# One set of four PSUM banks for the projections, the maxima and the down projection, in place of separate sets of one and three

## The chip, the cores and the metric

The kernel runs on one core of a Trainium2 chip. The metric is the device time in microseconds (us) of one execution. Names of the engines in this text: PE is TensorE's matmul queue (PEld is its weight load), DVE is VectorE, ACT is ScalarE, POOL is GpSimd, SP is SyncE, which issues the DMAs. The matmuls write to PSUM, of which there are eight banks here; a bank holds 128 x 512 fp32 values, and the engines that read it afterwards are DVE and ACT.

## The reference

One layer (DEPTH is 1) on 2048 tokens of width 1024:

```python
h = _modulate(x, ln1_g[l], sh1, sc1)
u = h @ w_in[l]
fq, fk, fv, fg, dq, dk, dv = jnp.split(u, splits, axis=-1)
...
fox_out = _fox_attention(fq, fk, fv, log_f)
...
diff_out = _diff_attention(dq[:, :, 0], dq[:, :, 1], dk[:, :, 0], dk[:, :, 1], dv, lam, slopes)
...
x = x + g1[:, None, :] * (mixed @ w_out[l])

h2 = _modulate(x, ln2_g[l], sh2, sc2)
y = (jax.nn.silu(h2 @ w_gate[l]) * (h2 @ w_up[l])) @ w_down[l]
x = x + g2[:, None, :] * y
```

Both attentions are causal and softmaxed; q and k are normalised per head. There are 8 heads of 64 in the first and 4 heads of two maps each in the second. The hidden width of the last product is 2816.

## The kernel before

**Precision.** Nearly every operand is split into two fp16 parts, a high and a low one, and each product is made as three matmuls (high x high, high x low, low x high) that add up in one bank.

**Start (about 0 to 150 us).** The modulation is computed, x is normalised block by block (16 blocks of 128 tokens), transposed on PE (L245, into banks of the tags "mx" and "st" in turn) and split into `hts`. The first blocks are projected (L451).

**Attention (about 150 to 1470 us).** There are eight groups: four differential ones, then four pairs of heads of the other kind. A group is 80 units; a unit is one block of 128 keys against 512 queries (`qc`, `kb`) of one of two maps `m`. For each unit `scores` writes to a bank "st" (L593, L594, and L596 for the mask), ACT takes the exponential out of it (L599) and copies it to fp16 (L604), POOL makes the low part (L607), and three units later (`PVLAG`) `weigh` multiplies with the values into a bank "pv" (L621 to L623). Ahead of the scores of a row of queries stand the maxima: `max_part` (L560) writes scores to a bank "mx", DVE reduces them (L562, or L564 on the diagonal), L569 makes the row `t_mrow`, L572 transposes it with four small matmuls and ACT puts it with the queries (L573).

**Between the units** PE projects for the next group: 16 blocks, each 24 matmuls into one bank "ip" (L451). ACT empties it in two copies (L452, L456) and DVE takes the low part of the values last (L144). During the last group it is the output projection that is done between the units (`out_proj`, L950, 24 matmuls into a bank, read by DVE in L952).

**Feed-forward (about 1600 us to the end).** In 22 rounds `product` makes seven products of 12 matmuls each for the gate and seven for the up weights (L1143, banks "st", "pv" and, for i = 6, "mx", which L1172 reads); `down` multiplies the round before with w_down, 6 matmuls into a bank "mx" (L1202), which DVE adds to the residual (L1206). Maxima over partitions are made with one matmul (`colmax`, L108, here into "ip") that DVE reduces (L109). Over the first ten rounds the rest of the normalised rows is made as well (`late_sum`). DVE also reduces each load of w_down (L1113).

**What sets the order.** The program is written as streams that are merged by weight (`run`). A scheduler then puts each engine's instructions into a fixed order; it gives a PSUM bank to a tile when one of its tag's set is free. On the chip every engine goes through its queue in that order and waits where an operand or a bank is not ready. So the number of banks of a tag acts twice: on the order that is written down, and on what is waited for.

Of the kernel before, what the change touches and what calls it, by code (L numbers as in the profile page):

```python
# [55 lines left out]
def trunk(ctx, tc, t):  # L56
# [5 lines left out]
    dram = ctx.enter_context(tc.tile_pool(name="dram", bufs=1, space=bass.MemoryType.DRAM))  # L62
    V, A, G, T = nc.vector, nc.scalar, nc.gpsimd, nc.tensor

    PSB = {"ip": 1, "st": 2, "pv": 2, "mx": 3}

    def bank(tag, dt=F32):
        n = 512 if dt == F32 else 1024
        return ps.tile([P, n], dt, tag=tag, bufs=PSB[tag], name=f"ps_{tag}")

    def small(n, tag, bufs=3, dt=F32):
# [28 lines left out]
    def colmax(am, tag=None):  # L100

        g = small(1, "cm", bufs=4)
        if tag is None:
            G.partition_all_reduce(g, am, channels=P, reduce_op=ReduceOp.max)
            return g

        b = bank(tag)
        T.matmul(b[:, 0:P], lhsT=am.broadcast_to([P, P]), rhs=idb, start=True, stop=True)  # L108
        V.tensor_reduce(out=g, in_=b[:, 0:P], op=ALU.max, axis=AX.X)  # L109
        return g  # L110
# [85 lines left out]
    def ada_columns(acc, q, ab):  # L196

        b = bank("ip")
        for i in range(KT):
            T.matmul(b[:, i : i + 1], lhsT=acc[:, i * P : (i + 1) * P], rhs=ones, start=(i == 0), stop=True, skip_group_check=True)  # L200
        bb = bada[:, q * KT : (q + 1) * KT]
        if q % 3 == 0:
            V.tensor_tensor(out=ab[:, KT:], in0=b[:, 0:KT], in1=bb, op=ALU.add)
        else:
            V.tensor_tensor(out=ab[:, 0:KT], in0=b[:, 0:KT], in1=bb, op=ALU.add)
            g = lng[:, (q // 3) * KT : (q // 3 + 1) * KT]
            V.scalar_tensor_tensor(out=ab[:, 0:KT], in0=ab[:, 0:KT], scalar=1.0, in1=g, op0=ALU.add, op1=ALU.mult)
# [29 lines left out]
    def to_hT(y, ab, s, ht, col, t32, tag="mx"):  # L237

        h = ht.bitcast(F16).rearrange("p (k s n) -> p k s n", k=KT, s=2)[:, :, :, col : col + P]
        t3 = t32.rearrange("p (k n) -> p k n", k=KT)  # L240
        for half in range(2):
            b = bank(tag)
            for i in range(4):
                k = half * 4 + i
                T.transpose(out=b[:, i * P : (i + 1) * P], in_=y[:, k * P : (k + 1) * P], identity=idf)  # L245
            for i in range(4):
                k = half * 4 + i
                if i < 3:
                    A.activation(t3[:, k, :], b[:, i * P : (i + 1) * P], AF.Identity, bias=ab[:, KT + k : KT + k + 1], scale=ab[:, k : k + 1])
                else:  # L250
                    V.tensor_scalar(out=t3[:, k, :], in0=b[:, i * P : (i + 1) * P], scalar1=ab[:, k : k + 1], scalar2=ab[:, KT + k : KT + k + 1], op0=ALU.mult, op1=ALU.add)
        cast_scaled("G", h[:, :, 0, :], t3, s)
        sub_scaled(h[:, :, 1, :], t3, s, h[:, :, 0, :])
# [1001 lines left out]
    for q in range(NQP + 1):  # L1255
        st = [[] for _ in range(14)]
# [109 lines left out]
```

## Time and profile before

| | |
|---|---|
| median of 3 runs | 2898.03 us (2892.18 to 2898.2) |
| profiled execution | 2903.69 us |
| its span | 2901.9 us |
| PE busy | 2717.1 us, 94% |
| DVE busy | 2143.8 us, 74% |
| ACT busy | 1436.7 us, 50% |
| POOL busy | 1655.5 us, 57% |

The span is what the profiler shows from the first to the last instruction; 1.8 us of the execution lie around it. A share is the time in which the engine had at least one instruction running. Matmuls overlap, so two that start 0.2 us apart can each last 0.4 us.

### The profile page before, as it was taken

What the parts mean: (1) busy time and instruction counts of PE and PEld (TensorE: products, weight loads), DVE (VectorE), ACT (ScalarE), POOL (GpSimd) and SP (SyncE); (2) the same over time, 40 slices, a digit from 0 to 9 for tenths busy, and PEclk for the clock granted to TensorE, in tenths of its full rate; (3) what the DMA queues carried; (4) which work ended last, traced back from release to release, by engine and by line L of the source; (5) the groups of instructions that cost most, each with busy time, mean ns of one, the idle gap of its engine ahead of it and who ended that gap; (6) DMA issues with size and microseconds to landing.
All of it is one profiled execution on the core that took longest, in us unless ns stands there. A gap on an engine that the chain in (4) does not pass through costs nothing. (4 is left out here: it accounts for less than half of the span.)

```text
span 2901.9 us, 49724 instructions
## 1 busy us (share of the span) xinstructions
PE 2717.1 (94%) x18924; PEld 1478.5 (51%) x18924; DVE 2143.8 (74%) x4195; ACT 1436.7 (50%) x2704; POOL 1655.5 (57%) x1392
## 2 busy tenths in 40 slices
PE   4899989899998999999899899999999999999999
PEld 3466656566665655665444344444444444444444
DVE  7786675867758686646766887878877787878785
ACT  4666667666676777786552432333323232333231
POOL 2566666665667787776552655555554545455541
PEclk9999999999999999999999999999999999999999
DMA  6332231322223244225678333333334511111111
GB/s 233 77 90 56 63 76 39 84 49 67 74 50 91 53 112 96 49 55 158 165 185 257 122 114 100 97 106 102 106 97 153 174 58 59 59 44 64 53 37 58
DMA packets 276816, 274.52 MB, mean 95 GB/s; under 512 B 205144, under 2 KB 221912, under 8 KB 270816
## 3 DMA queue, kind: packets, MB, share of 16 engines
q1 hardware_dynamic: 276576, 271.34, 33.2%
q8 instruction: 148, 2.42, 0.4%
q14 instruction: 92, 0.75, 0.1%
HBM read 181.94 MB, written 41.11 MB: 77 GB/s over the span
## 5 line engine op out<-in xcount | busy, mean ns | idle before, releaser
L607 POOL TENSOR_TENSOR pxs<-pxs 128x512 f16<-128x512 f32 (+3 forms) x640 | 685.1, 1085 | 333.1 <-ACT pxs L604 200.7
L451 PE MATMUL ps_ip<-wbuf,ht 128*128 128x384 f16 (+1 forms) x2952 | 563.2, 333 | 24.4 <-DVE vts L144 14.4
L1143 PEld LDWEIGHTS <-mt 128*128 128x128 f16 x3696 | 358.4, 98 | 437.2 <-issue 14.4
L1202 PE MATMUL ps_mx<-wide,ht 128*128 128x512 f16 x2112 | 505.5, 380 | 21.5 <-DVE mt L1206 16.1
L1087 POOL TENSOR_TENSOR pxm<-vts 128x512 f32<-128x512 f32 x220 | 342.5, 1588 | 211.0 <-DMA vts<-in_w_gu_dram 200.7
L599 ACT ACTIVATE pxs<-ps_st,cells 128x512 f32<-128x512 f32 (+3 forms) x640 | 388.7, 620 | 141.1 <-PE ps_st L594 69.4
L451 PEld LDWEIGHTS <-ht 128*128 128x128 f16 x3072 | 296.7, 100 | 241.5 <-issue 47.3
L1143 PE MATMUL ps_st<-ht,mt 128*128 128x512 f16 x1584 | 373.5, 379 | 0.1
L1143 PE MATMUL ps_pv<-ht,mt 128*128 128x512 f16 x1584 | 368.6, 379 | 0.0
L604 ACT ACTIVATE pxs<-pxs 128x512 f16<-128x512 f32 (+3 forms) x640 | 350.6, 565 | 18.9 <-PE ps_pv L623 10.2
L621 PE MATMUL ps_pv<-vts,pxs 128*128 128x129 f16 (+1 forms) x2176 | 342.2, 207 | 4.7 <-DVE os L640 3.7
L1202 PEld LDWEIGHTS <-ht 128*128 128x128 f16 x2112 | 205.2, 98 | 274.4 <-issue 25.2
L622 PE MATMUL ps_pv<-vts,pxs 128*128 128x128 f16 (+1 forms) x2176 | 344.2, 208 | 0.0
L623 PE MATMUL ps_pv<-vts,pxs 128*128 128x129 f16 (+1 forms) x2176 | 324.9, 206 | 7.7 <-POOL pxs L607 7.0
L562 DVE TENSOR_REDUCE t_mxc<-ps_mx 128x1 f32<-128x512 f32 x384 | 256.7, 682 | 91.1 <-PE ps_mx L560 89.5
L1206 DVE SCALAR_TENSOR_TENSOR mt<-ps_mx,t_ai,mt 128x512 f32<-128x512 f32 x352 | 256.3, 742 | 34.2 <-PE ps_mx L1202 34.0
L621 PEld LDWEIGHTS <-pxs 128*128 128x128 f16 x2176 | 207.9, 97 | 56.8 <-ACT pxs L599 3.5
L593 PE MATMUL ps_st<-mt 67*128 67x512 f16 (+7 forms) x640 | 223.5, 350 | 11.3 <-ACT pxs L599 10.9
L623 PEld LDWEIGHTS <-pxs 128*128 128x128 f16 x2176 | 206.6, 99 | 45.7 <-POOL pxs L607 18.5
L622 PEld LDWEIGHTS <-pxs 128*128 128x128 f16 x2176 | 207.7, 97 | 35.7 <-issue 4.5
L594 PE MATMUL ps_st<-mt 128*128 128x512 f16 (+3 forms) x640 | 223.3, 349 | 0.0
L560 PE MATMUL ps_mx<-mt 71*128 71x512 f16 (+7 forms) x640 | 197.1, 349 | 17.2 <-DVE t_mxc L562 12.5
(262 smaller groups left out, 4136.6 us busy)
## 6 DMA issues: line engine op xcount, KB each, us to landing
vts<-in_w_gu_dram SPq DMA_DIRECT2D x44, 1024.0 KB
stg<-in_w_down_dram SPq DMA_DIRECT2D x44, 512.0 KB
stg<-in_w_ada_dram SPq DMA_DIRECT2D x32, 512.0 KB
stg<-in_w_in_dram SPq DMA_DIRECT2D x24, 512.0 KB
stg<-yd SPq DMA_DIRECT2D x48, 256.0 KB
mt<-in_w_ada_dram SPq DMA_DIRECT2D x16, 512.0 KB
mt<-mt SPq DMA_DIRECT2D x128, 64.0 KB
mixed<-os SPq DMA_DIRECT2D x32, 256.0 KB
```

The lines of the kernel that those rows point to most:

```text
L451: T.matmul(pt[:, 0:N], lhsT=h4[:, k, hs, c : c + P], rhs=w4[k // 4][:, k % 4, ws, 0:N], start=(i == 0), stop=(i == len(terms) - 1))
L562: V.tensor_reduce(out=mx[:, 4 * j + n : 4 * j + n + 1], in_=b[:, 0:w], op=ALU.max, axis=AX.X)
L599: A.activation(p32[:, c0:QC], b[:, c0:QC], AF.Exp, bias=pshift, scale=1.0)
L604: A.activation(ph[:, c0:QC], p32[:, c0:QC], AF.Copy, bias=0.0, scale=1.0)
L607: (V if hilo[1] == "V" else G).tensor_tensor(out=pl[:, c0:QC], in0=p32[:, c0:QC], in1=ph[:, c0:QC], op=ALU.subtract)
L621: T.matmul(pv[:, jj, :], lhsT=lhs_h, rhs=v4[:, kb, h, 0 : W + 1], start=first, stop=False, skip_group_check=True)
L622: T.matmul(pv[:, jj, 0:W], lhsT=lhs_h, rhs=v4[:, kb, h, W + 2 : 2 * W + 2], start=False, stop=False, skip_group_check=True)
L623: T.matmul(pv[:, jj, :], lhsT=lhs_l, rhs=v4[:, kb, h, 0 : W + 1], start=False, stop=end, skip_group_check=True)
L1087: G.tensor_tensor(out=sums[:, k * 512 : (k + 1) * 512], in0=raw[:, a * 512 : (a + 1) * 512], in1=raw[:, b * 512 : (b + 1) * 512], op=op)
L1143: T.matmul(b.rearrange("p (b n) -> p b n", b=4), lhsT=aw[w][:, APOS[i] * 4 + k, ws, :], rhs=cb[:, :, 2 * k + hb, :], start=(fresh and k == ...
L1202: T.matmul(b, lhsT=aT[:, th, as_, f, j * P : (j + 1) * P], rhs=dnb[:, (2 * q + f) % 4, ws, n * 512 : (n + 1) * 512], start=(f == 0 and z = ...
L1206: V.scalar_tensor_tensor(out=xs, in0=b, scalar=sets[q]["ai", th], in1=xs, op0=ALU.mult, op1=ALU.add)
```

## The change

The bank table loses the tags "ip" (one bank) and "mx" (three) and gains "any" (four); `bank` maps every tag that the table does not have to "any". The tags "st" and "pv" keep their two banks each, so all eight banks are in use before and after. No instruction is added or removed; all lines below L65 move down by one.

```diff
-    PSB = {"ip": 1, "st": 2, "pv": 2, "mx": 3}
+    PSB = {"any": 4, "st": 2, "pv": 2}
 
     def bank(tag, dt=F32):
         n = 512 if dt == F32 else 1024
+        tag = tag if tag in PSB else "any"
         return ps.tile([P, n], dt, tag=tag, bufs=PSB[tag], name=f"ps_{tag}")
```

The scheduler writes another order for every engine. Three places follow.

**PE at the start**, from the matmul that gives the bound of the modulation to the first projection (`ht` is the normalised block at L245 and the transposed one at L451). Before:

```order
L108 LDWEIGHTS t_amh
L108 MATMUL ps_mx<-idb,t_amh 128x128
L245 MATMUL ps_mx<-idf,ht 128x128 x8
L451 LDWEIGHTS ht
L451 MATMUL ps_ip<-wbuf,ht 128x392
```

After:

```order
L109 LDWEIGHTS t_amh
L109 MATMUL ps_any<-idb,t_amh 128x128
L246 MATMUL ps_any<-idf,ht 128x128 x8
L246 MATMUL ps_st<-idf,ht 128x128 x8
L246 MATMUL ps_any<-idf,ht 128x128 x8
L452 LDWEIGHTS ht
L452 MATMUL ps_any<-wbuf,ht 128x392
```

The transposes of the second and third block stood behind 16 and 19 matmuls of the first projection, and now stand ahead of it.

**PE in the attention** of the fourth group (qc = 1, the second map), at the scores of its third to fifth block of keys; the numbers are those of the tiles, the same in both orders. Before, from the score tile 9536:

```order
L451 MATMUL ps_ip_9741<-wbuf_100,ht_239 128x384
L593 LDWEIGHTS mt_7152
L593 MATMUL ps_st_9536<-mt_7152 128x512
L594 LDWEIGHTS mt_7152
L594 MATMUL ps_st_9536<-mt_7152 128x512
L560 LDWEIGHTS mt_7149
L560 MATMUL ps_mx_9518<-mt_7149 128x512
L593 LDWEIGHTS mt_7152
L593 MATMUL ps_st_9573<-mt_7152 128x512
```

After, from the same tile to the start of 9618, the next one:

```order
L594 MATMUL ps_st_9536<-mt_7152 128x512
L595 LDWEIGHTS mt_7152
L595 MATMUL ps_st_9536<-mt_7152 128x512
L594 LDWEIGHTS mt_7152
L594 MATMUL ps_st_9573<-mt_7152 128x512
L595 LDWEIGHTS mt_7152
L595 MATMUL ps_st_9573<-mt_7152 128x512
L594 LDWEIGHTS mt_7152
L594 MATMUL ps_st_9618<-mt_7152 128x512
```

Before, the two matmuls of 9573, three of the maxima and 12 of the weighting stand between the scores 9536 and 9618, two tiles apart on a set of two banks; now only the two matmuls of 9573 do.

**DVE in the feed-forward**, around the reduction of the first load of w_down for the twelfth round (`t_dam<-stg`); the lines after the change are higher by one. Before:

```order
L1157 TENSOR_TENSOR uhm<-ps_st,uhm 128x512
L1206 SCALAR_TENSOR_TENSOR mt<-ps_mx,t_ai,mt 128x512 x2
L1166 TENSOR_TENSOR mt<-ps_pv,pxm 128x512
L1113 TENSOR_REDUCE t_dam<-stg 128x1
L1206 SCALAR_TENSOR_TENSOR mt<-ps_mx,t_ai,mt 128x512
L123 TENSOR_REDUCE t_amh<-uhm 128x1
L1206 SCALAR_TENSOR_TENSOR mt<-ps_mx,t_ai,mt 128x512
L109 TENSOR_REDUCE t_cm<-ps_ip 128x1
```

After:

```order
L1158 TENSOR_TENSOR uhm<-ps_st,uhm 128x512
L1207 SCALAR_TENSOR_TENSOR mt<-ps_any,t_ai,mt 128x512 x2
L1167 TENSOR_TENSOR mt<-ps_pv,pxm 128x512
L1114 TENSOR_REDUCE t_dam<-stg 128x1
L1207 SCALAR_TENSOR_TENSOR mt<-ps_any,t_ai,mt 128x512
L124 TENSOR_REDUCE t_amh<-uhm 128x1
L1207 SCALAR_TENSOR_TENSOR mt<-ps_any,t_ai,mt 128x512
L110 TENSOR_REDUCE t_cm<-ps_any 128x1
```

Nothing moved here; only the set of banks is another.

## Rows read from the trace of the kernel before

**Rows 1.** The page: the span and the busy times of the engines.

```profile
span 2901.9 us, 49724 instructions
...
PE 2717.1 (94%) x18924; PEld 1478.5 (51%) x18924; DVE 2143.8 (74%) x4195; ACT 1436.7 (50%) x2704; POOL 1655.5 (57%) x1392
```

**Rows 2.** Busy time by stretch: length, the engines, granted clock, DMA share, GB/s.

```profile
60.00:150.00 90.00, 72.86 (x466) 45.21 (x465) 67.97 (x178) 58.66 (x163) 51.59 (x52) 0.92 0.26 66
...
300.00:1300.00 1000.00, 941.98 (x9147) 611.09 (x9144) 692.08 (x1710) 695.98 (x1500) 679.13 (x696) 0.98 0.29 69
1300.00:1670.00 370.00, 334.69 (x2326) 166.53 (x2325) 260.08 (x408) 185.85 (x342) 199.24 (x154) 0.97 0.64 176
1670.00:2310.00 640.00, 616.62 (x2860) 277.39 (x2859) 515.48 (x807) 201.32 (x236) 335.50 (x209) 0.99 0.38 117
2310.00:2902.00 592.00, 585.87 (x2747) 266.41 (x2744) 457.08 (x730) 173.02 (x193) 277.57 (x167) 1.00 0.16 55
```

**Rows 3.** What PE waited for: us in total, times, longest.

```profile
PE ps_ip L200 <- DVE ht L194: 22.9, 2, 14.1
PE ps_mx L1202 <- DVE mt L1206: 16.1, 18, 2.2
PE ps_mx L572 <- DVE t_mrow L569: 15.6, 11, 2.5
PE ps_ip L451 <- DVE vts L144: 14.4, 14, 2.9
PE ps_ip L950 <- DMA wide<-wide: 13.0, 5, 6.8
PE ps_mx L560 <- DVE t_mxc L562: 12.5, 20, 1.6
...
PE ps_st L593 <- ACT pxs L599: 10.9, 17, 2.1
...
PE ps_mx L1143 <- DVE mt L1206: 5.0, 3, 3.9
PE ps_ip L950 <- DVE uhm L952: 4.7, 5, 1.9
...
PE ps_mx L560 <- DVE t_mxc L564: 3.3, 2, 3.0
PE ps_ip L950 <- DVE ht L952: 3.3, 4, 1.8
```

**Rows 4.** DVE in order of time around 2180 us: start, us, instruction, [idle before].

```profile
2172.82 0.67 DVE L1166 TENSOR_TENSOR mt<-ps_pv,pxm 128x512 f32<-128x512 f32 x1
2180.60 1.22 DVE L1113 TENSOR_REDUCE t_dam<-stg 128x1 f32<-128x1024 f32 x1 [7.10 <-DMA stg<-in_w_down_dram]
2181.74 0.74 DVE L1206 SCALAR_TENSOR_TENSOR mt<-ps_mx,t_ai,mt 128x512 f32<-128x512 f32 x1
...
2184.18 0.28 DVE L109 TENSOR_REDUCE t_cm<-ps_ip 128x1 f32<-128x128 f32 x1
```

**Rows 5.** PE in order of time in the feed-forward, at three places.

```profile
1741.81 2.72 PE L1202 MATMUL ps_mx<-wide,ht 128*128 128x512 f16 x6 [2.21 <-DVE mt L1206]
...
1780.80 1.45 PE L1202 MATMUL ps_mx<-wide,ht 128*128 128x512 f16 x6 [1.15 <-DVE mt L1206]
...
2171.70 2.75 PE L1202 MATMUL ps_mx<-wide,ht 128*128 128x512 f16 x12
2174.28 0.22 PE L108 MATMUL ps_ip<-idb,t_amh 128*128 128x128 bf16 x1
```

**Rows 6.** The start in order of time, PE and POOL.

```profile
43.04 5.41 PE L451 MATMUL ps_ip<-wbuf,ht 128*128 128x392 f16 x16 [5.79 <-POOL ht L141]
...
43.56 3.27 POOL L235 TENSOR_SCALAR ht<-ht,t_nr 128x1024 f32<-128x1024 f32 x2 [0.57 <-DVE t_eps L379]
...
48.24 1.27 PE L245 MATMUL ps_st<-idf,ht 128*128 128x128 f32 x8
```

**Rows 7.** The attention's score tiles from 300 to 1300 us, in groups.

```profile
L599 ACT ACTIVATE pxs<-ps_st,cells 128x512 f32<-128x512 f32 (+1 forms) x483 | 294.1, 620 | 102.5 <-PE ps_st L594 44.5 <-PE ps_pv L623 24.2 <-PE ps_st L596 20.9
```

## The prediction, made before the changed kernel was run

> **What bounds the kernel now.** I read the page first, then busy time by stretch, PE's list of waits, the order of time at the longest waits, and the written order of both kernels. PE runs for 94% of the span and no other engine above 74% [rows 1], so PE is the bound, and what a change of banks can give back is PE's idle time: 2901.9 - 2717.1 = 184.8 us. By stretch [rows 2]: in the attention 58 of 1000 us (300 to 1300), around the output projection 35 of 370, in the first half of the feed-forward 23 of 640, in its second half 6 of 592. That half runs almost without gaps at the full granted clock (1.00); in the other stretches the clock averages 0.92 to 0.99, so some matmuls also ran at 1.2 GHz instead of 2.4.
>
> The waits name what can be freed [rows 3]. Waits for a bank, that is for the reader of an older tile: 16.1 + 5.0 us for L1206 in the feed-forward, 14.4 us for L144 (a projection's only bank), 12.5 + 3.3 us for the maxima's L562 and L564, and 4.7 + 3.3 us for L952 after an output projection. That is 59 us. Waits that no bank of this set removes: 22.9 us at the start, 15.6 us for the row `t_mrow`, 13.0 us for transposes by DMA, and 10.9 us of score matmuls for the exponential that still reads their "st" bank.
>
> **The change part by part.** Counts of instructions and durations stay; banks and order change. The whole effect is in which gaps close and which open. I sum against the profiled execution, 2903.69 us, which is 5.66 us above the median of the runs; the same gain is taken off the median.
>
> *Feed-forward, gain 12 us.* A down tile is 6 matmuls; six at full clock take 1.45 us and twelve 2.75 [rows 5], so a further bank lets PE run on by 6 x 0.217 = 1.3 us before it has to wait. The 21 waits for L1206 average 1.0 us, so a fourth bank that was always free would close most of them. Why they arise is seen at 2180 us [rows 4]: DVE stands 7.10 us at L1113 for a load of w_down, and the next L1206 is queued behind it; PE uses up its three banks and then waits 3.9 us, the longest of its kind. The written DVE order at that place is the same before and after, so the block stays. And the fourth bank isn't free there: the column maximum that PE wrote at 2174.28 [rows 5] is read by L109 only at 2184.18, behind the same L1113. It had a bank of its own; now it takes one of the four. So the set helps while no column maximum is waiting. I take half of the 21.1 us, 10, and 2 us for matmuls that now stay at the high clock: after a gap of 2.21 us six took 2.72 us, after one of 1.15 us 1.45 [rows 5]. Bounds: 0, and 21.1 plus the 6 us that a mean clock of 0.99 costs over 640 us, so 27.
>
> *Output projection, gain 5 us.* In the new order the bank that a block of L950 takes was last written at least 2 us of PE work earlier, and in half of the cases over 10 us (count over the whole order; the half was 3.3 us with the one bank). The 8.0 us for L952 should go. But the block that starts sooner needs its transposed rows sooner, and those waits (13.0 us) are for DMA, in the stretch where DMA is busiest, 0.64 [rows 2]. I take 5; bounds 0 and 8.
>
> *Attention, loss 3 us.* With one bank a projection could start only when the one before was read, which spread the 24 matmuls over 48 matmuls on the average; now it is 38, and 45 of 128 projections run without a break, where 13 did. Of the 30 us of waits for L144, L562 and L564 I take 10 as gained, since the projections and maxima that run sooner meet each other in the same four banks: counted over the order, the number of projections with under 1.5 us of PE work since their bank's last write (oldest bank first) rises from 3 to 15, that of maxima from 29 to 34. Against that stands what the projections no longer cover. The stretch after the last projection of a group has only scores, maxima and weighting, and the order written there is tight: in the place shown, score 9618 follows 9536 after 2 x 0.217 us of PE work, while the exponential that must read the bank between them takes 0.62 us [rows 7]. Places with under 1.25 us of PE work between scores that share a bank: 8 before, 50 after. Waits for that exponential average 10.9/17 = 0.64 us; a place that short costs between 0 and that, I take 0.2: 42 x 0.2 = 8. Rows `t_mrow` with under 2 us of PE work after their last maximum: 1 before, 16 after; their waits average 15.6/11 = 1.4 us, and I take a quarter, 15 x 0.35 = 5. Sum: -10 + 8 + 5 = +3. Bounds: -30 (all bank waits gone, nothing new), and with every new place at the full mean and nothing gained 42 x 0.64 + 15 x 1.4 = +48.
>
> *Start, loss 2 us.* The first projection began at 43.04 and issued 16 matmuls, while POOL still scaled the next two blocks (two instructions, 43.56 to 46.83) [rows 6]. Now PE goes through both blocks' transposes first, so the projection starts some 5 us later, at about 48, and the transposes (1.27 us in the row for one block) are then already done. A part of this is repaid before 150 us, since PE is idle there for 17 of 90 us [rows 2]. I take 2; bounds 0 and 5.
>
> The order of SP's queue changes too, with the same DMAs; in the attention DMA is at 0.29 [rows 2], so I cost it at nothing. If a load of projection weights came late there, PE would meet it at a column maximum.
>
> Sum: -12 - 5 + 3 + 2 = -12: 2891.7 for the profiled execution's kind, 2898.03 - 12 = **2886** for the median.
>
> The Trainium skill (Perfetto Trace Analysis, section Matmuls) says that independent groups of matmuls should rotate through different banks, so that the reading of one overlaps the next. By it alone the 59 us go. The waits for `t_mrow` and for the score banks in this trace are of the kind that it doesn't reach.
>
> **The rivals.**
> 1. *All bank waits close.* PE waits 59 us for banks; if four shared banks always have a free one and nothing opens elsewhere, 2898 - 59 = 2839, less where the clock stays up. For it: projections and maxima rarely need all four at once. Against it: the scheduler has used the freedom to pack tighter, so slack per bank hardly rises. Take 2840 to 2865 as its region.
> 2. *Attention loses more than the rest gains.* The single projection bank kept projections spread, as filler for the chain of score, exponential and weighting. If the 42 tight scores and 15 tight rows cost their full mean, the attention loses 48 us, against 17 gained: 2898 + 31 + 2 = 2931. It decides from the point where the new waits at L594 and L573 pass the 27 us or so that bank waits give back (12 + 5 + 10). For it: the counts above, and one stretch of this kind in every group. Against it: what runs late there ran sooner elsewhere, and PE's total work is the same. The Trainium skill (TensorE: Matmul & The Clock Gate, section on psum-queue depth-cycling) describes many short idles between groups that cycle through banks, with the clock falling back and forth; the trace agrees so far as six matmuls took 2.72 us after a gap.
> 3. *Nothing that can be measured.* The tags seldom collide, gaps only change place, and the sum stays within 6 us of 2898.
>
> **How the numbers follow.** A measurement of this kernel tells about 0.2%, 5.8 us, from no change. Chances: my forecast, a small gain (2865 to 2892), 0.42; rival 1, 0.10; rival 3, 0.23; rival 2, 0.25, of which about half ends under 2912. So faster 0.52, same 0.22, slower 0.26. The likeliest case alone is 2865 to 2892; with both signs the range is 2862 to 2912.
>
> **What would show it.** Right: waits of L1203 and L1144 for L1207 fall from 21 us to about 10, the longest staying near 4 us at a load of w_down; waits of L951 for L953 nearly vanish and those for the DMA transposes grow; waits of L594 for L600 grow from 10.9 to about 19 and those of L573 from 15.6 to about 20; the first projection starts near 48 us. Wrong: if idle time in 300 to 1300 us falls well under 50 us, the tight places cost nothing and rival 1 is near; if it rises over 80, rival 2. If the second half of the feed-forward, which has almost no gaps to close, changes its length of 592 us, something that I don't see has moved.

## The result and the profile after

The changed kernel takes 2943.57 us (median of 4 runs, 2938.37 to 2945.77), the kernel before 2896.0 us in the same measurement: a ratio of 1.0139, 95% interval 1.0117 to 1.0161. It is slower by 1.4%, where a gain of 0.4% was predicted; the time lies above the predicted range of 2862 to 2912 us.

The page of the changed kernel, span and busy times:

```profile
span 2944.0 us, 49661 instructions
...
PE 2737.6 (93%) x18924; PEld 1489.3 (51%) x18924; DVE 2161.0 (73%) x4195; ACT 1427.2 (48%) x2704; POOL 1579.9 (54%) x1392
```

Against [rows 1], PE is busy for 20.5 us more with the same 18924 matmuls, and idle for 206.4 us instead of 184.8. So of the 42 us by which the span grew, half is added idle time and half is added busy time of the same matmuls.

To see where, the span is cut at the same points of the work in both kernels: the first score of the attention, the first score of the last (eighth) group, the first gate product, and the start of the twelfth round of the feed-forward. Busy time by stretch, columns as in [rows 2], the kernel before:

```profile
0.00:129.20 129.20, 80.55 (x437) 50.94 (x438) 98.18 (x246) 64.09 (x175) 52.78 (x57) 0.95 0.51 174
129.20:1306.60 1177.40, 1106.01 (x10637) 721.62 (x10636) 813.08 (x2007) 817.36 (x1771) 795.27 (x810) 0.99 0.29 68
1306.60:1592.90 286.30, 260.01 (x1939) 132.32 (x1937) 194.04 (x312) 148.53 (x290) 140.43 (x119) 0.96 0.70 191
1592.90:2244.10 651.20, 618.79 (x2865) 277.24 (x2864) 528.35 (x819) 212.23 (x254) 357.17 (x222) 0.99 0.36 110
2244.10:2901.90 657.80, 651.77 (x3055) 296.43 (x3053) 510.17 (x815) 194.47 (x217) 309.87 (x186) 1.00 0.21 69
```

The changed kernel:

```profile
0.00:137.50 137.50, 74.80 (x422) 49.96 (x423) 99.74 (x249) 64.31 (x175) 52.31 (x57) 0.90 0.48 162
137.50:1349.40 1211.90, 1121.68 (x10622) 728.42 (x10620) 833.45 (x1997) 810.56 (x1769) 793.09 (x810) 0.97 0.27 66
1349.40:1657.80 308.40, 272.44 (x1969) 138.12 (x1968) 198.35 (x318) 149.56 (x292) 137.81 (x119) 0.92 0.68 178
1657.80:2289.00 631.20, 617.58 (x2863) 276.57 (x2863) 520.56 (x820) 211.33 (x253) 326.34 (x222) 0.99 0.37 114
2289.00:2944.00 655.00, 651.08 (x3055) 296.27 (x3053) 508.87 (x815) 191.48 (x217) 270.40 (x186) 1.00 0.20 69
```

The lengths give the balance: start +8.3, groups 0 to 6 +34.5, last group with the output projection +22.1, feed-forward -20.0 and -2.8. Three stretches lose, and in each of them the granted clock is lower as well (0.95 to 0.90, 0.99 to 0.97, 0.96 to 0.92). The feed-forward gains nearly twice what was predicted. The halves of the 42 us are sums of unlike parts: PE's idle time and busy time change by +14.0 and -5.8 us at the start (where 15 matmuls moved to later stretches), by +18.8 and +15.7 in groups 0 to 6, by +9.7 and +12.4 in the last group, and by -20.9 and -1.9 in the feed-forward.

What PE waited for in the changed kernel (us, times, longest; lines are higher by one), over the whole span:

```profile
PE ps_any L109 <- DVE t_amh L124: 31.7, 17, 12.2
PE ps_any L573 <- DVE t_mrow L570: 25.5, 21, 3.0
PE ps_st L594 <- ACT pxs L600: 23.7, 29, 3.1
...
PE ps_any L951 <- DMA wide<-wide: 13.2, 2, 12.2
...
PE ps_any L1144 <- DVE mt L1207: 0.8, 1, 0.8
```

The largest of these was 12.3 us before. It is the column maximum of a load of weights (L109), which waits for the reduction of those weights (L124):

```profile
PE ps_mx L108 <- DVE t_amh L123: 12.3, 4, 4.2
```

In groups 0 to 6 alone, the kernel before (rows and diagonal maxima, 15.6 and 3.3 us, have all their waits here and stand in [rows 3]):

```profile
PE ps_ip L451 <- DVE vts L144: 14.1, 13, 2.9
PE ps_mx L560 <- DVE t_mxc L562: 12.0, 19, 1.6
PE ps_st L593 <- ACT pxs L599: 9.9, 14, 2.1
```

And the changed kernel there:

```profile
PE ps_any L573 <- DVE t_mrow L570: 21.9, 18, 3.0
PE ps_any L561 <- DVE t_mxc L563: 18.4, 16, 4.5
PE ps_st L594 <- ACT pxs L600: 16.8, 25, 2.6
...
PE ps_any L561 <- DMA mt<-mt: 7.5, 7, 2.7
PE ps_any L561 <- DVE vts L145: 4.7, 3, 3.0
PE ps_any L452 <- DVE t_mxc L563: 4.0, 7, 1.6
PE ps_any L561 <- DVE t_mxc L565: 2.8, 5, 1.3
PE ps_any L452 <- DVE vts L145: 1.4, 3, 0.9
```

Beside [rows 3]: the 21.1 us of waits for L1207 are gone but for 0.8 us, and the wait for the transposes by DMA, 13 us in both, now comes almost in one piece of 12.2. In groups 0 to 6 the projections' wait for the read of the projection before them fell from 14.1 to 1.4 us, but 4.0 us of waiting for maxima came instead, and the maxima's waits for banks went from 15.3 (12.0 + 3.3) to 25.9 (18.4 + 4.7 + 2.8), three of them for a bank that a projection holds. Rows (L573) went from 15.6 to 21.9, scores behind the exponential (L594) from 9.9 to 16.8.

One entry is new. Maxima wait 7.5 us for a DMA into `mt`, the tile with the queries and keys that are made from the projections. Such waits, 3.4 to 9.0 us in all, stand in each of the seven kernels of this text whose projections can't run ahead, and in none of the five others. This fits projections that come late and hold up the maxima that read them.

The start shows what such a wait does. PE in order of time, the kernel before:

```profile
105.62 0.23 PE L108 MATMUL ps_mx<-idb,t_amh 128*128 128x128 bf16 x1 [2.59 <-DVE t_amh L123]
106.10 5.82 PE L451 MATMUL ps_ip<-wbuf,ht 128*128 128x392 f16 x24 [0.25 <-DVE fgl L459]
111.75 0.22 PE L108 MATMUL ps_mx<-idb,t_amh 128*128 128x128 bf16 x1
116.15 0.23 PE L108 MATMUL ps_mx<-idb,t_amh 128*128 128x128 bf16 x1 [4.17 <-DVE t_amh L123]
```

And the changed kernel:

```profile
106.01 0.23 PE L109 MATMUL ps_any<-idb,t_amh 128*128 128x128 bf16 x1 [3.43 <-DVE t_amh L124]
108.99 0.29 PE L109 MATMUL ps_any<-idb,t_amh 128*128 128x128 bf16 x1 [2.75 <-DVE t_amh L124]
121.45 0.29 PE L109 MATMUL ps_any<-idb,t_amh 128*128 128x128 bf16 x1 [12.18 <-DVE t_amh L124]
...
121.72 6.64 PE L452 MATMUL ps_any<-wbuf,ht 128*128 128x392 f16 x24
```

Before, a projection ran between two of these maxima and filled a part of the time in which the next load was reduced. Now all three come first and the projection stands behind them: PE idles for 2.75 and 12.18 us with 24 matmuls in its queue. The Trainium skill (PSUM — Partial Sum Buffer, section Engine vs sequencer instructions) says that matmuls start and complete in program order; the trace agrees: the projection starts at 121.72, behind the last of the three, where it started at 106.10 before.

### The profile page after: what moved, and what is told of

Its sections match the earlier page's. It is cut to its first block, busy times and chain, and to the rows that moved or that the text cites. A ratio compares the mean times of both kernels' runs of the same rounds, so it can differ in the third digit from the quotient of the medians.

```text
span 2944.0 us, 49661 instructions
## 1 busy us (share of the span) xinstructions
PE 2737.6 (93%) x18924; PEld 1489.3 (51%) x18924; DVE 2161.0 (73%) x4195; ACT 1427.2 (48%) x2704; POOL 1579.9 (54%) x1392
## 4 chain that ended last, share of the span: by engine, by line
PE 50%; DVE 22%; DMA 13%; POOL 5%; ACT 4%; issue 4%; SPq 1%; POOLq 0%; DVEq 0%; ACTq 0%
PE ps_any L452 10%; PE ps_any L1203 10%; PE ps_pv L1144 7%; PE ps_st L1144 7%; PE ps_any L951 3%; DMA vts<-in_w_gu_dram 2%; DVE t_mxc L563 2%; PE ps_any L1144 2%; DMA stg<-in_w_ada_dram 2%; PE ps_st L594 2%; DVE mt L145 2%; PE ps_st L595 2%; PE ps_any L561 2%; DVE mt L1207 2%; PE ps_pv L624 2%
## 5 line engine op out<-in xcount | busy, mean ns | idle before, releaser
L608 POOL TENSOR_TENSOR pxs<-pxs 128x512 f16<-128x512 f32 (+3 forms) x640 | 673.3, 1068 | 374.7 <-ACT pxs L605 239.7
L452 PE MATMUL ps_any<-wbuf,ht 128*128 128x384 f16 (+1 forms) x2952 | 549.5, 336 | 6.1 <-DVE t_mxc L563 4.0
L1203 PE MATMUL ps_any<-wide,ht 128*128 128x512 f16 x2112 | 504.1, 379 | 1.9 <-DVE ht L145 0.8
L1088 POOL TENSOR_TENSOR pxm<-vts 128x512 f32<-128x512 f32 x220 | 292.6, 1362 | 242.5 <-DMA vts<-in_w_gu_dram 235.9
L1144 PE MATMUL ps_st<-ht,mt 128*128 128x512 f16 x1584 | 382.3, 379 | 1.9 <-ACT mt L1147 1.9
L624 PE MATMUL ps_pv<-vts,pxs 128*128 128x129 f16 (+1 forms) x2176 | 327.0, 207 | 11.4 <-POOL pxs L608 10.7
L563 DVE TENSOR_REDUCE t_mxc<-ps_any 128x1 f32<-128x512 f32 x384 | 257.2, 682 | 96.3 <-PE ps_any L561 95.4
L1207 DVE SCALAR_TENSOR_TENSOR mt<-ps_any,t_ai,mt 128x512 f32<-128x512 f32 x352 | 258.3, 744 | 42.0 <-PE ps_any L1203 41.8
L594 PE MATMUL ps_st<-mt 67*128 67x512 f16 (+7 forms) x640 | 227.2, 355 | 24.7 <-ACT pxs L600 23.7
L140 ACT ACTIVATE mt<-pxm,t_ws 128x1536 f16<-128x1536 f32 x88 | 119.3, 1359 | 252.6 <-DVE t_p2b L119 115.6
L561 PE MATMUL ps_any<-mt 71*128 71x512 f16 (+7 forms) x640 | 201.5, 359 | 42.2 <-DVE t_mxc L563 20.1
L624 PEld LDWEIGHTS <-pxs 128*128 128x128 f16 x2176 | 208.6, 99 | 55.8 <-POOL pxs L608 25.9
L622 PEld LDWEIGHTS <-pxs 128*128 128x128 f16 x2176 | 209.7, 98 | 49.5 <-ACT pxs L605 5.2
```

What stands on the lines that cost most here:

```text
L452: T.matmul(pt[:, 0:N], lhsT=h4[:, k, hs, c : c + P], rhs=w4[k // 4][:, k % 4, ws, 0:N], start=(i == 0), stop=(i == len(terms) - 1))
L563: V.tensor_reduce(out=mx[:, 4 * j + n : 4 * j + n + 1], in_=b[:, 0:w], op=ALU.max, axis=AX.X)
L608: (V if hilo[1] == "V" else G).tensor_tensor(out=pl[:, c0:QC], in0=p32[:, c0:QC], in1=ph[:, c0:QC], op=ALU.subtract)
L622: T.matmul(pv[:, jj, :], lhsT=lhs_h, rhs=v4[:, kb, h, 0 : W + 1], start=first, stop=False, skip_group_check=True)
L624: T.matmul(pv[:, jj, :], lhsT=lhs_l, rhs=v4[:, kb, h, 0 : W + 1], start=False, stop=end, skip_group_check=True)
L1088: G.tensor_tensor(out=sums[:, k * 512 : (k + 1) * 512], in0=raw[:, a * 512 : (a + 1) * 512], in1=raw[:, b * 512 : (b + 1) * 512], op=op)
```

## The experiments

The points in the table are those of the two fences above, and the start of the fourteenth round, from which the distance of the changed kernel moves by under 1 us. Each is given as the difference to the kernel before in the profiled executions (us, cumulated from the start of the span); the last columns are the median and the ratio to the kernel before.

| kernel | first score | first score of last group | first gate product | start of round 14 | median | ratio (95%) |
|---|---|---|---|---|---|---|
| changed kernel | +8.3 | +42.8 | +64.9 | +42.9 | 2943.57 | 1.0139 (1.0117 to 1.0161) |
| separate, then shared | -1.7 | -4.1 | -4.6 | -26.0 | 2880.02 | 0.9927 (0.9908 to 0.9946) |
| shared, then separate | +8.7 | +37.3 | +47.6 | +60.0 | 2966.78 | 1.0233 (1.0216 to 1.0251) |
| shared, projections paced | +8.7 | +36.9 | +59.4 | +40.5 | 2944.91 | 1.0154 (1.0135 to 1.0174) |
| shared, maxima at most 3 | +8.6 | +45.7 | +67.0 | +45.9 | 2942.28 | 1.0148 (1.0129 to 1.0166) |
| shared, both limits | +8.4 | +47.1 | +63.4 | +38.8 | 2938.39 | 1.0126 (1.0096 to 1.0157) |
| separate, one order | +8.6 | +56.2 | +96.8 | +104.4 | 3008.13 | 1.0375 (1.0349 to 1.0401) |
| projections' own bank, others share 3 | -0.2 | -2.9 | +19.4 | +4.6 | 2920.64 | 1.0075 (1.0047 to 1.0102) |
| separate, projections hold | +7.3 | +50.8 | +47.5 | +45.9 | 2947.94 | 1.0154 (1.0134 to 1.0175) |
| separate, maxima hold | -1.5 | +1.2 | +18.8 | +19.9 | 2925.35 | 1.0081 (1.0060 to 1.0101) |
| shared from the last row of queries | -2.1 | +0.8 | +7.6 | -16.7 | 2881.01 | 0.9926 (0.9910 to 0.9942) |

The medians come from four measurements, in which the kernel before took 2896.0, 2898.99, 2896.97 and 2903.5 us; kernels of different measurements are best compared by their ratios.

**Gain and loss taken apart.** Two pools in turn; the sets change ahead of the last six of the 16 blocks of the output projection. (A block is two half-blocks of 24 matmuls; the expectations of this run and of the one with one order say "tenth half-block" for the tenth block, and the last one "half-blocks 4 to 9" for the blocks 6 to 9.)

```diff
+    SPLIT, SHARED = {"ip": 1, "mx": 3}, {"any": 4}
+    set_banks(SPLIT)
...
+    set_banks(SHARED)
     run(outs[10:12])
```

The second kernel has the two calls the other way round.

> Separate sets (one and three banks) until the tenth half-block of the output projection, the shared four from there and through the feed-forward. PE's written order is that of the kernel before up to there, and that of the changed kernel behind it. Theory A (the loss lies in the order and the waits of start, attention and output projection; the gain of the feed-forward is that of a fourth bank for its down tiles): the attention is that of before, the first half of the feed-forward 20 us shorter, the second 3, so about 2896 - 22 = 2874. Rival B (the feed-forward gained only because the attention had left it work, or a higher clock): no gain alone, 2890 to 2900. Rival C (the loss sits in the feed-forward's neighbourhood, at the change from one stage to the other): over 2900.

> The reverse: the shared four through start, attention and output projection, and separate sets of one and three from there on. PE's written order is that of the changed kernel up to there. Theory A (the two halves are independent): the loss of about 65 us at the start of the feed-forward stays and its gain of 22 goes: 2943.6 + 22 = 2965. Rival B (the feed-forward's gain doesn't come from its banks): 2940 to 2948. The two runs of this pair should add up to before plus after: 2874 + 2965 = 2896 + 2943.

Measured: 2880.02 and 2966.78, the numbers of theory A within 6 and 2 us. The ratios multiply to 0.9927 x 1.0233 = 1.016, the changed kernel's 1.014 within the intervals: in the medians the two halves add up. The second number is in part luck, since its parts are not those expected. The loss at the first gate product is 47.6 us and not about 65: the last group cost +10.3 us where it cost +22.1 in the changed kernel. And the feed-forward, expected as before, took 1321.9 us, 12.9 more than in the kernel before. The feed-forward of the first of the two, in the same columns as above:

```profile
1588.30:2220.10 631.80, 615.30 (x2863) 275.52 (x2863) 520.95 (x820) 211.12 (x253) 323.64 (x222) 1.00 0.36 113
2220.10:2875.10 655.00, 651.05 (x3055) 296.30 (x3053) 509.14 (x815) 191.24 (x217) 269.02 (x186) 1.00 0.20 69
```

Both lengths are those of the changed kernel to 0.6 us, behind an attention that lost nothing. This kernel beats both. The gain holds over the table: the feed-forward takes 1283.6 to 1289.3 us in all six kernels that share the four banks there, and 1307.4 to 1321.9 us in the five that keep one and three.

**First theories of the loss: spacing and number.** In `pace` a projection's first matmul is made to depend on the DVE read of the projection before; in the other kernel a maximum's tile depends on the read of the third tile before it (MAXLIVE is 3); the third kernel has both.

```diff
+                if i == 0 and (g or blk >= 4 * FIRST):
+                    pace(mm)
...
+        if len(maxima) >= MAXLIVE:
+            tc.add_manual_dep(mm.ins, maxima[-MAXLIVE].ins.name, mybir.DependencyInfo(mybir.DependencyClass.Sync, mybir.DependencyReason.DATA), reason="limit")
```

> The shared four, with each projection from the second group on told to wait for the read of the one before, as a single bank made it. Theory T1 (the loss comes from projections that are no longer spaced by their one bank): the 42 us of the attention come back mostly, 2943.6 - 30 to - 42, so 2900 to 2915. Rival T3 (the projections come late because the maxima take all four banks first, and then run in a clump; spacing them doesn't bring them earlier): within 10 us of 2944. In the written order a projection's 24 matmuls are spread over 35 matmuls with this edit (38 in the changed kernel, 48 before), which speaks for T3.

> The shared four, but the maxima and their transposed row may hold only three banks at a time, so that they leave one to the projections. Theory T3 (maxima that run ahead take the banks): the waits of projections and maxima for one another (12 us in the changed kernel) go, and the attention comes back by some 20 to 40 us: 2905 to 2925. Theory T1 (spacing of the projections): no change, 2938 to 2948.

> The shared four with both limits of the two earlier runs: projections wait for the read of the one before, and maxima hold three banks at most. What the four banks may hold is then nearly what the separate sets held; only the program order of one set remains. Theory T4 (that order is the cause): no recovery, 2935 to 2955. Rival (spacing and number together, each alone being too little): 2900 to 2920.

Measured: 2944.91, 2942.28 and 2938.39. By their ratios (1.0154, 1.0148 and 1.0126) none is told from the changed kernel's 1.0139. What the four banks may hold at a time, made nearly the same as in the separate sets, changes nothing that can be measured. So T1 falls as far as it said that a projection must wait for the read of the one before, and T3 as far as it said that the maxima's number is the cause. The written spread did not come back with the pacing (35 matmuls, 48 before), so this alone doesn't say what a wider spread would do; below, one bank for the projections goes with a spread of 37 and of 49, as they may run ahead or not.

**The theory that was left.** The written order of PE shows it when the tiles are numbered as the program names them. In these kernels a set's tiles begin strictly in that order: 271 tiles of "ip", 1153 of "mx" before, 1424 of "any" after, not one exchanged. Between two sets there is no such rule, and before there were 183 places where one set had passed the other: 82 of the 123 projections in these sets began ahead of their place (by 2.9 tiles as the mean of all 123, by 17 at most), and half-blocks of the output projection up to 19 behind. In the changed kernel there are none. So one set is also one queue.

The test keeps the separate banks and fixes the order alone, up to the tenth block of the output projection.

```diff
+    def one_order():
+        seen, last = set(), None
+        for i in nc.cur_bb.bb.instructions:
...
+                if name.startswith(("ps_ip", "ps_mx")) and name not in seen:
+                    if last is not None:
+                        tc.add_manual_dep(i, last, mybir.DependencyInfo(mybir.DependencyClass.NoSync, mybir.DependencyReason.DATA), reason="one order")
+                    seen.add(name)
+                    last = i.name
...
+    one_order()
     run(outs[10:12])
```

> The banks of the kernel before (one and three, separate), but PE is told to begin the tiles of both sets in the order in which the program names them, up to the tenth half-block of the output projection; no wait is added, only the order is fixed. Reason: within a set the scheduler begins tiles strictly in program order. With two sets there are 183 places of 1424 tiles where one set has overtaken the other (82 of 123 projections begin earlier than their place, by 2.9 tiles on the average); with one set there is none. Theory T4 (the loss is this coupling: projections can't overtake maxima that aren't ready, nor be overtaken): attention and output projection lose as in the changed kernel, the feed-forward stays as before, so 2950 to 2970. Rival B (tiles that share banks wait for each other's readers): the banks are still separate, so about the time of before, 2890 to 2910.

Measured: 3008.13, beside 2896.97 of the kernel before in the same measurement. The order alone, with no bank shared, costs 111 us, more than the 2950 to 2970 expected. It loses in the same stretches as the changed kernel, by the same at the start (+8.6) and by more behind it: groups 0 to 6 +47.6, the last group +40.6, and the feed-forward +7.6 where the shared set gains. Why it loses more is not shown. One part can be seen: it keeps one bank for the output projection and takes its freedom to fall behind the maxima, and PE waits 9.4 + 5.8 us for that bank (4.7 + 3.3 before):

```profile
PE ps_ip L961 <- DVE ht L963: 9.4, 5, 3.2
PE ps_ip L961 <- DVE uhm L963: 5.8, 3, 2.8
```

The counterpart gives freedom back: the projections have a set of their own, all other tiles share three banks.

```diff
-    PSB = {"any": 4, "st": 2, "pv": 2}
+    PSB = {"own": 1, "any": 3, "st": 2, "pv": 2}
...
-            pt = bank("ip" if g or blk >= 4 * FIRST else PTAGS[blk % len(PTAGS)])
+            pt = bank("own" if g or blk >= 4 * FIRST else PTAGS[blk % len(PTAGS)])
```

> The projections alone have a bank of their own, everything else (maxima, rows, column maxima, transposes, output projection, down products) shares three. Theory T4: the projections overtake again (82 of 123 begin ahead of their place, by 3.6 tiles), a projection's 24 matmuls are spread over 49 matmuls again (48 before, 38 in the changed kernel), so the attention up to the last group is as before; the output projection is still coupled to the maxima, so the last group keeps its loss of about 22 us; the feed-forward has three banks and gains little or nothing: 2915 to 2925. Rival B (it is the sharing of banks as such, now by more kinds of tiles on three banks): as slow as the changed kernel or slower, 2940 to 2970.

Measured: 2920.64, within the numbers of T4, and by stage as it said: groups 0 to 6 take 1174.70 us (1177.40 before), the last group loses 22.2, and the feed-forward is 3.9 us shorter as a whole. (Its +4.6 at round 14 flatters: 50 matmuls that the kernel before has done by then are still to come, and the end is +15.5.)

```profile
129.00:1303.70 1174.70, 1109.35 (x10634) 724.40 (x10633) 816.43 (x2002) 817.50 (x1769) 792.25 (x811) 0.98 0.28 68
1303.70:1612.20 308.50, 265.35 (x1945) 135.49 (x1942) 198.92 (x318) 150.22 (x290) 138.41 (x119) 0.92 0.67 178
```

**Which of the two may not be held.** The forced order again on separate banks, one direction at a time: a tile of "ip" waits its turn behind the "mx" tiles named ahead of it, or the reverse.

```diff
-                    if last is not None:
+                    seen.add(name)
+                    if name.startswith("ps_mx"):
+                        last = i.name
+                    elif last is not None:
...
-                    seen.add(name)
-                    last = i.name
```

This is the first kernel; the second has "ps_ip" in the third line.

> Separate banks as before; only one half of the forced order: a tile of the projections' set may not begin before the tiles of the maxima's set that the program names ahead of it, while maxima may still pass projections. A projection is then spread over 37 matmuls (before 48, changed kernel 38). Theory T4a (what is lost in groups 0 to 6 is the projections' lead, with which they filled the places where maxima weren't ready): first score of the last group 35 to 55 us later than before, the last group itself within 10 us of before; in all 2935 to 2955. Rival T4b (what is lost is that maxima stand behind projections): within 10 us of before, 2890 to 2910.

> The other half: maxima may not begin before the projections' tiles that the program names ahead of them, while projections may still run ahead (spread over 49 matmuls, as before). T4a: start and groups 0 to 6 within 10 us of before, and the loss comes in the last group, where the half-blocks of the output projection, up to 19 tiles behind their place in the kernel before, can't be passed any more: 20 to 45 us there, 2915 to 2945 in all. Rival T4b: the loss of 35 to 55 us stands in groups 0 to 6 already.

Measured: 2947.94 and 2925.35, within the numbers of T4a in both; only the 17.5 us of the second kernel's last group fall short of the 20 to 45 expected. Groups 0 to 6 and the last group of the first, then of the second:

```profile
136.40:1357.40 1221.00, 1132.42 (x10652) 735.00 (x10651) 834.31 (x2003) 809.72 (x1771) 793.06 (x812) 0.96 0.26 66
1357.40:1640.40 283.00, 260.36 (x1942) 133.88 (x1939) 188.59 (x313) 148.64 (x289) 134.97 (x116) 0.96 0.73 193
```

```profile
127.60:1307.80 1180.20, 1102.62 (x10632) 719.47 (x10631) 808.18 (x1999) 815.14 (x1771) 800.83 (x812) 0.99 0.27 68
1307.80:1611.60 303.80, 265.22 (x1942) 133.26 (x1941) 191.91 (x320) 149.03 (x290) 134.20 (x118) 0.96 0.69 180
```

Projections that can't run ahead cost 43.6 us in groups 0 to 6 (1221.0 against 1177.4) and nothing in the last group (283.0 against 286.3). Maxima that can't pass cost 2.8 us there and 17.5 in the last group, where the output projection is what they would pass.

**A better place to change sets?** The sets change earlier, ahead of the last row of queries.

```diff
+    set_banks(SHARED)
     run(flat(last[ends[2] :]), norm_pair(1) + outs[6:8] + norm_pair(2) + outs[8:10] + norm_pair(3))
...
-    set_banks(SHARED)
     run(outs[10:12])
```

> As the first run (separate, then shared), but shared already from the last row of queries of the last group on, so that the half-blocks 4 to 9 of the output projection also use four banks. Theory T4: half-blocks are no longer behind maxima there by much, their waits for the one bank (8 us for L952 before) go: 0 to 6 us less than the first run, 2872 to 2880, which the measurement can just not tell apart. Rival: maxima or rows of the last two maps are held up by half-blocks that wait for DMA, 2885 to 2905.

Measured: 2881.01, one microsecond off the first version and the same in ratio (0.9926 and 0.9927), so the run doesn't tell the two apart, and the gain of 0 to 6 us was not found. In its profiled execution the first gate product comes 12 us later against the kernel before than in the first version (+7.6 against -4.6); in the medians nothing of that is left.

## Why the prediction was wrong, point by point

**The step that failed** is that of the attention, in the sentence on what a projection's one bank does: it took the new order as the old one packed tighter, and priced it by places that are short (42 at 0.2 us, 15 at 0.35) less 10 us of bank waits. The term was +3; it measured +34.5, inside its bounds of -30 to +48. What was read there, a projection spread over 48 matmuls before and 38 after, was the sign of something else: a set is a queue, and by joining two sets the change took from the projections the right to begin before maxima that were not ready. This could have been seen before any run, by asking of the written order which tiles had passed which. The prediction looked at distances in it, not at exchanges.

**In the terms of that sum** (-10 for bank waits, +8 for tight scores, +5 for tight rows), read in groups 0 to 6: the two prices were right as a sum: scores behind the exponential rose by 6.9 us (16.8 - 9.9) and rows by 6.3 (21.9 - 15.6), 13.2 for 13. (Over the whole span they rose by 12.8 and 9.9.) What failed is the -10 and what was put at nothing. The bank waits of projections and maxima did not fall, they went from 29.4 (14.1 + 12.0 + 3.3) to 31.3 us (18.4 + 4.7 + 4.0 + 2.8 + 1.4). Maxima waited 7.5 us for the queries and keys of late projections, and the weighting (L624) 4.7 us more for POOL; other waits fell by some 8 to 9. That makes the added idle time of 18.8 us. The other 15.7 us of the 34.5 are busy time.

**The clock** was not in the sum for the attention: 15.7 us in groups 0 to 6 and 12.4 in the last group, at a granted clock of 0.97 for 0.99 and 0.92 for 0.96. Two projections in the last group of the changed kernel, in order of time on PE, show how:

```profile
1360.55 3.57 PE L452 MATMUL ps_any<-wbuf,ht 128*128 128x384 f16 x21
...
1368.35 0.19 PE L622 MATMUL ps_pv<-vts,pxs 128*128 128x65 f16 x1 [1.53 <-DVE os L634]
...
1370.12 0.58 PE L561 MATMUL ps_any<-mt 71*128 71x512 f16 x1 [1.55 <-DVE t_mxc L563]
...
1374.70 5.61 PE L452 MATMUL ps_any<-wbuf,ht 128*128 128x384 f16 x19
```

Before the two gaps a matmul of a projection takes 3.57/21 = 0.17 us, behind them 5.61/19 = 0.30. Three stretches, the first run of these matmuls, from the first gap's end to the second run, and the second run, with the granted clock as the third figure from the end:

```profile
1360.55:1364.00 3.45, 3.45 (x24) 2.08 (x23) 2.42 (x8) 0.89 (x5) 2.33 (x4) 1.00 0.99 396
1368.35:1374.70 6.35, 4.41 (x27) 2.21 (x27) 5.43 (x17) 4.80 (x9) 5.65 (x6) 0.57 0.00 1
1374.70:1380.10 5.40, 5.40 (x20) 2.65 (x19) 1.09 (x3) 1.23 (x3) 3.85 (x4) 0.56 0.78 209
```

It is 1.00 before the gaps, that is 2.4 GHz, and 0.56 behind them, nearly all at 1.2 GHz. 3.1 us of waiting went with some 2.4 us of longer matmuls in the second projection alone (19 x 0.125). This fits the balance of the attention with its last group, where 28.5 us of added idle time came with 28.1 of added busy time. It is no rule for the kernel: the feed-forward lost 20.9 us of idle time and only 1.9 of busy time.

**Output projection:** -5 predicted (0 to -8), +22.1 measured for the last group with it. The waits for L953 went as said, from 8.0 to 1.6 us, and the DMA's longest grew from 6.8 to 12.2. But the loss lies elsewhere: 20.3 of the 22.1 us are there by the last score, at 1587.5 us, and the wait of 12.2 comes behind it, at 1613. What was missed is the order between half-blocks and maxima. The runs show it from both sides: with only the projections freed the loss stays (+22.2 with the projections' own bank), with only the maxima held it comes back (+17.5), and with only projections and half-blocks held there is none (283.0 against 286.3). Which single waits carry it is less clear. In the changed kernel the maxima wait only 0.9 us for the read of a half-block; what grew in the last group are their waits for other maxima (0.5 to 7.4 us), those of scores for the exponential (1.0 to 6.9), and the busy time. (The forecast called this the stretch where DMA is busiest, at 0.64; of those in [rows 2] it is, but the first 60 us have 0.74.)

**Start:** +2 predicted (0 to 5), +8.3 measured. The first projection began at 48.4 us, as forecast from the order, and that cost nothing: the kernel with the projections' own bank begins it at 48.5 and has its first score at 129.0 us, where the kernel before has 129.2. The loss stands at the 12.18 us wait at 121.45 us (4.17 before), a place at which the forecast didn't look: the longest of its kind is 12.0 to 12.2 us in all seven kernels whose projections can't run ahead, and 3.6 to 4.2 us in the five where they can.

**Feed-forward:** the right mechanism, the size off: -12 predicted, -22.8 measured, inside the bounds of 0 to -27. Of these, 1.9 us are busy time, as forecast (2), and 20.9 are idle time, for 10. The failed step is "I take half", since the column maximum was to hold the fourth bank. The place of [rows 4], now 45 us later, on DVE and then on PE:

```profile
2225.53 1.22 DVE L1114 TENSOR_REDUCE t_dam<-stg 128x1 f32<-128x1024 f32 x1 [6.36 <-DMA stg<-in_w_down_dram]
```

```profile
2220.87 0.22 PE L109 MATMUL ps_any<-idb,t_amh 128*128 128x128 bf16 x1
...
2224.81 1.46 PE L1144 MATMUL ps_st<-ht,mt 128*128 128x512 f16 x6
2228.59 0.23 PE L109 MATMUL ps_any<-idb,t_amh 128*128 128x128 bf16 x1 [2.33 <-DVE t_amh L124]
```

DVE stands at the load for 6.36 us, as before, and the maximum of 2220.87 does hold a bank. But PE has other work until 2226, and when it stops it stops at the next column maximum, for 2.33 us, not for L1207. The Trainium skill's rule on rotating groups through banks (Perfetto Trace Analysis, section Matmuls), which the prediction weighed, agrees here: 21.1 us of such waits became 0.8. That it is the number of banks alone is not shown: with the projections' own bank the down products share three banks, and their waits for L1207 are 0.5 us as well, but they wait 10.5 us for an operand (L145) instead, and the feed-forward gains 3.9 us.

**Of the rivals** the second came true, at 2943.6, where it gave 2931 with a chance of 0.25. Its mark, idle time from 300 to 1300 us over 80, was all but reached: PE is busy there for 921.9 of 1000 us. Its mechanism was half right: the projections are the filler and lose their place. But the 48 us that it put on tight scores and rows measured 13.2 in groups 0 to 6 and 22.7 in all, so that its number came near is luck; and one bank doesn't space the projections by itself, since they have it in the kernel "projections hold" too, with a spread of 37. What the prediction did get: the first projection at 48, L953's waits nearly gone, L594 and L573 growing (to 23.7 and 25.5, for 19 and 20), and a second half of the feed-forward that hardly changes (655.0 for 657.8). The transposes' wait for DMA, which was to grow, stayed at 13 us in total.

What stays open: why the kernel with one order loses 111 us where its two directions apart lose 44 and 22 (2947.94 and 2925.35 against 2903.5 in their measurement); the 7 us by which the bank waits shown there grew are a small part of it. Open too is why separate sets in the feed-forward took 12.9 us more behind a shared attention than in the kernel before.

## What to carry to other kernels

A set of PSUM banks is two things at once: room, and, under a scheduler that begins a set's tiles in program order, a queue. Joining sets gives room and takes the freedom of one kind of work to pass another; before joining, count in the written order where one kind passes the other, and ask which of them is the filler for the other's waits. Where stages differ, change the sets between them: separate sets as long as projections fill gaps, one set where all tiles come in step, gave 0.7% here.

## What the runs showed that was not expected

Short waits can cost about as much again in the clock: two gaps of 1.5 us went with matmuls of 0.30 us in place of 0.17 in the next projection, and in the attention with its last group 28.5 us of added idle time came with 28.1 us of added busy time. That a projection begins 5 us later costs nothing at the start (129.0 against 129.2 us at the first score), while the 12.18 us wait with a projection standing behind it, for one of 4.17, goes with 8.3 us lost.
